# Memory keys by pairs of features, products of zeros at the start, and a fixed TensorE order in the first stage of an encoder kernel

## The chip, the cores and the metric

The kernel runs on one core of a Trainium2 chip. The metric is the device time of one execution in microseconds (us). A core has five engines that run side by side, each through its own list of instructions in order: PE (TensorE, matrix products; PEld is its weight load), DVE (VectorE), ACT (ScalarE), POOL (GpSimd) and SP (SyncE, which here only issues transfers). Transfers run on 16 DMA engines that all queues share. Data lives in SBUF, products accumulate in eight PSUM banks of 128 x 512 numbers.

## The reference, cut to what matters

One layer of an encoder on two sequences of 512 tokens (`x_prompt`, `x_sample`, 1024 features), each with its own memory of 256 tokens.

```
xn = rmsnorm(x, norm_mix);  mn = rmsnorm(mem, norm_mem)
u, q, k, v, xq, g = split(xn @ w_in)
y_s5   = s5_branch(u, lambda, log_step, b, c, ...)      # state-space scan in both directions
y_diff = diff_attention(rope(q), rope(k), v)
mk, mv = split(mn @ w_mem_kv)                           # keys and values of the memory
y_x    = cross_attention(xq, mk, mv)
merged = sum_n sigmoid(g_n) * (branch_n @ w_up[n])
x = x + merged @ w_out
x = x + ffn(rmsnorm(x));  out = rmsnorm(x)
```

All of it is float32. The change touches only what comes first: `mk`, `mv`, the norm of `x`, the product that gives `u`, and the small coefficients of the S5 branch (powers of exp(lambda * step) and the scaled `b`).

## The kernel before, in words

**Number format.** Every large product is done in three: an operand is split into a high part (a cast, ACT, line 122 or 125) and a low part (what is left, DVE, line 123 or 126), and `hi*hi + hi*lo + lo*hi` is accumulated. `weight` (131-137) loads 512 KB of weights into `wf` (two buffers), and `split` makes `wh` and `wl` (two buffers each). `mm3` (141-149) issues the three products of one 128-row slice. All PE instructions of the main program have line 55 (products) or 58 (transposes), since they pass through the class `InOrder`; while its flag `on` is set, each instruction it issues is held to the order of the program.

**Who sets the order.** The Tile framework plans at compile time the order of each engine's list with a simulated clock: an instruction that is ready goes, and among ready ones the earlier in the program. `tc.issue_after(ins)` puts what its block issues behind `ins` on `ins`'s engine. `queued()` (270) does so behind the last weight transfer on SP, `yielding(sp)` (275) behind a split's cast on ACT and its subtraction on DVE.

**First stage, lines 204-335.** The memory arrives transposed in four tiles `mt` of two feature slices each (`mem_part`, 210), is scaled and split into `mh`, `ml`. The keys come head by head: `mem_k(h, w)` (245) needs all eight feature slices and one weight tile, adds 24 products in one PSUM bank of the tag "tr", and ACT copies the bank out (line 252). The weights `w_mk` are laid out for that by `_mtiles` (1413). The values come by pairs of features: `mem_v(c, w)` (257) needs one `mh`/`ml` tile and one weight tile for 24 products into four banks of the tag "mm", kept open over four calls.

Beside them the norm of `x` is prepared. `sums` (216) loads tokens (`tk`) and lets ACT square and add them (line 223). `factor` (183) takes the root on ACT (186) and the reciprocal on DVE (187), and spreads it with four PE transposes (190, shown with line 58) over a "tr" bank. `x_norm` (233) makes `xh` and `xl` from it, with three instructions for each of 16 slices (lines 237-239).

**S5.** `s5_gen` is a generator; each `next(s5)` issues a part of it. Its second part loads `lr`, `li`, `ls` (1110-1112). Its third, issued at line 336 behind `uw`, loads `br`, `bi`, `cr`, `cn` (1116-1119), computes the small coefficients in some 90 DVE instructions on 128 x 32 numbers (1080-1199), and then the input weights (`cprod` on DVE 1237-1239, transposes on PE 1251). After the products of `u` (line 350, banks "mm") come the output weights (PE 1283), the state inputs (PE 1312), the scan of 62 steps on DVE (1327-1330) and the outputs (PE 1355-1357), which line 376 puts behind the twelfth gate product on PE. Gate products (`gates`, 361) fill PE meanwhile.

The first lines of the stage's order:

```python
mem_part(0)
mw = [weight(a["w_mk"][0])]
for i in range(1, 4):
    mem_part(i)
mw.append(weight(a["w_mk"][1]))
with queued():
    next(s5)
    ss0 = sums(a["xN"][0], ts=range(3))
mem_k(0, mw[0])
```

Of the kernel before, what the change touches and what calls it, by code (L numbers as in the profile page):

```python
# [19 lines left out]
P = 128  # L20
L = 512
# [40 lines left out]
def encoder(ctx: ExitStack, tc: tile.TileContext, a, out):  # L62
# [4 lines left out]

    cst = ctx.enter_context(tc.tile_pool(name="cst", bufs=1))
    edge = ctx.enter_context(tc.tile_pool(name="edge", bufs=1, side="right"))
    V.memset(edge.tile([P, 248], F32, name="pad_r"), 0.0)  # L70
# [23 lines left out]
    def slot(tag, shape=(P, NT), dt=F32, name="sl"):  # L94
        return pools[tag].tile(list(shape), dt, tag=tag, name=name)
# [4 lines left out]
    def aux():  # L100
        return bank("tr")


    ident = cst.tile([P, P], F32, name="ident")
    nc.sync.dma_start(ident, a["ident"])
    vec = cst.tile([P, N_VEC], F32, name="vec")
    nc.sync.dma_start(vec, a["vecs"])
    onec = cst.tile([P, 2], F32, name="onec")
# [5 lines left out]
    def vcol(name, i=0):  # L114
        o = VEC[name][0] + i
        return vec[:, o : o + 1]


    def split(hi, lo, src, scale=None):

        if scale is None:
            h = S.copy(hi, src)  # L122
            l_ = V.tensor_tensor(out=lo, in0=src, in1=hi.bitcast(F32), op=ALU.subtract)  # L123
        else:
            h = S.activation(out=hi, in_=src, func=AF.Copy, scale=scale)
            l_ = V.scalar_tensor_tensor(out=lo, in0=src, scalar=scale, in1=hi.bitcast(F32), op0=ALU.mult, op1=ALU.subtract)
        return h, l_
# [54 lines left out]

    def factor(ss, n, nt=4, bias=epsc):

        rs = rp.tile([P, 4], F32, tag="rs", name="rs", bufs=4)
        S.activation(out=rs[:, :nt], in_=ss[:, :nt], func=AF.Sqrt, scale=1.0 / n, bias=bias)
        V.reciprocal(rs[:, :nt], rs[:, :nt])
        bc = aux()
        for t in range(nt):
            PE.transpose(bc[:, t * P : (t + 1) * P], rs[:, t : t + 1].broadcast_to([P, P]), ident)  # L190
        return rs, bc

# [17 lines left out]
    def mem_part(i):  # L210
        mt_ = slot("ld", [P, 2, L], name="mt")
        nc.sync.dma_start(mt_, a["memT"][:, 2 * i : 2 * i + 2, :])
        for j in range(2):
            split(mh[i][:, j, :], ml[i][:, j, :], mt_[:, j, :], scale=vcol("norm_mem", 2 * i + j))

    def sums(src, tag="wb", ss=None, ts=range(4)):

# [22 lines left out]

    mhk = [mh[i // 2][:, i % 2, :] for i in range(KD)]
    mlk = [ml[i // 2][:, i % 2, :] for i in range(KD)]
    mf = None

    def mem_k(h, w):
        nonlocal mf
        o = aux()
        for i in range(KD):
            mm3([o], *w, [(mhk[i], mlk[i])], i, KD)
        if h % 2 == 0:  # L250
            mf = slot("ld", [P, 2, L], name="mf")
        S.copy(mf[:, h % 2], o)
        return mf

    ob = []
# [24 lines left out]
    mem_part(0)  # L280
    mw = [weight(a["w_mk"][0])]
    for i in range(1, 4):
        mem_part(i)
    mw.append(weight(a["w_mk"][1]))
    with queued():
        next(s5)
        ss0 = sums(a["xN"][0], ts=range(3))
    mem_k(0, mw[0])
    mw.append(weight(a["w_mk"][2]))
    with queued():  # L290
        sums(a["xN"][0], ss=ss0, ts=(3,))
        x_load(0, range(2))
    mf0 = mem_k(1, mw[1])
    mw.append(weight(a["w_mk"][3]))
    with queued():
        x_load(0, range(2, 4))
        ss1 = sums(a["xN"][1], ts=range(1))
    _, bc = factor(ss0, DM)
    with yielding(last_s):
        x_norm(0, bc, range(2))  # L300
    mem_k(2, mw[2])
    mw.append(weight(a["w_mv"][0]))
    with queued():
        sums(a["xN"][1], ss=ss1, ts=range(1, 4))
    with yielding(last_s):
        x_norm(0, bc, range(2, 6))
    mf1 = mem_k(3, mw[3])
    mw.append(weight(a["w_mv"][1]))
    with queued():
        x_load(1)  # L310
    with yielding(last_s):
        x_norm(0, bc, range(6, 8))
        _, bc = factor(ss1, DM)
        x_norm(1, bc, range(2))
    mem_v(0, mw[4])
    mw.append(weight(a["w_mv"][2]))
    with yielding(last_s):
        x_norm(1, bc, range(2, 6))
    s5_from = last_s
    mem_v(1, mw[5])  # L320
    mw.append(weight(a["w_mv"][3]))
    with queued():
        nc.sync.dma_start(mD[0], mf0)
        nc.sync.dma_start(mD[1], mf1)
    with yielding(last_s):
        x_norm(1, bc, range(6, 8))
    mem_v(2, mw[6])
    mem_v(3, mw[7])
    for s in range(NS):
        mf = slot("ld", [P, 2, L], name="mf")  # L330
        for j in range(2):
            S.copy(mf[:, j], ob[2 * s + j])
        nc.sync.dma_start(mD[2 + s], mf)
    uw = [weight(a["w_in"][t]) for t in range(2)]
    with tc.issue_after(s5_from[0].ins):
        next(s5)

# [4 lines left out]
    for t2 in range(2):  # L342
        if t2:
            uw = [weight(a["w_in"][2 + t]) for t in range(2)]
        us = [slot("ld", [P, T, NS, NC], name="ut") for _ in range(2)]
        for s in range(NS):
            for t in range(2):
                o = bank()
                for k in range(KD):
                    mm3([o], *uw[t], [x_of(k, s)], k, KD)  # L350
                S.copy(us[t][:, :, s, :], o.rearrange("p (j c) -> p j c", c=NC))
        for t in range(2):
            nc.sync.dma_start(uD[(2 * t2 + t) * P : (2 * t2 + t + 1) * P], us[t])
# [742 lines left out]
def s5_gen(k):  # L1096
# [14 lines left out]
    nc.sync.dma_start(li, a["lam_im"])  # L1111
    nc.sync.dma_start(ls, a["log_step"])
    yield
    br, bi = pp.tile([P, G, 16], F32, name="br"), pp.tile([P, G, 16], F32, name="bi")
    cr, cn = cp.tile([P, G, 16], F32, name="cr"), cp.tile([P, G, 16], F32, name="cn")
    nc.sync.dma_start(br, a["b_re"])
    nc.sync.dma_start(bi, a["b_im"])
    nc.sync.dma_start(cr, a["c_re"])
    nc.sync.dma_start(cn, a["c_im"])

    def sm(nm, n=G):
        return pp.tile([P, n], F32, tag="m_" + nm, name=nm)
# [75 lines left out]
    V.tensor_tensor(out=gr, in0=gr, in1=dn, op=ALU.mult)  # L1198
    V.tensor_tensor(out=gi, in0=gi, in1=dn, op=ALU.mult)


    V.tensor_scalar_mul(cn, cn, -1.0)
    b_r, b_i = cp.tile([P, G, 16], F32, name="b_r"), cp.tile([P, G, 16], F32, name="b_i")
# [196 lines left out]
def layout(i):  # L1400
    i = {k_: np.asarray(v_) for k_, v_ in i.items()}
    a = {}
    x = np.stack([_tok(i["x_prompt"][0]), _tok(i["x_sample"][0])])
    a["xT"] = x.reshape(NS, L, KD, P).transpose(0, 3, 2, 1)
    mem = np.concatenate([i["mem_prompt"][0], i["mem_sample"][0]])
    a["xN"] = x.reshape(NS, 4, P, DM)
    a["memN"] = mem.reshape(4, P, DM)
    a["memT"] = mem.reshape(2 * NMEM, KD, P).transpose(2, 1, 0)
    w = i["w_in"][0]
    a["w_in"] = _mtiles(w)  # L1410
    a["w_v"] = np.stack([_moving(w[:, 1536 + 256 * h : 1792 + 256 * h], 4) for h in range(2)])
    wk = i["w_mem_kv"][0]
    a["w_mk"] = _mtiles(wk[:, :512])
    a["w_mv"] = _moving(wk[:, 512:], 2)
    a["w_glu"] = _mtiles(i["s5_w_glu"][0])
    a["w_up"] = np.stack([_mtiles(i["w_up"][0, n]) for n in range(3)])
    a["w_out"] = _mtiles(i["w_out"][0])
    a["w_fg"] = _mtiles(i["w_ffn_in"][0][:, :FF])
    a["w_fu"] = _mtiles(i["w_ffn_in"][0][:, FF:])
    a["w_fo"] = _mtiles(i["w_ffn_out"][0])  # L1420
    vecs = {"norm_mix": i["norm_mix"][0], "norm_mem": i["norm_mem"][0], "norm_ffn": i["norm_ffn"][0],
            "norm_final": i["norm_final"], "s5_d": i["s5_d"][0], "s5_b_glu": i["s5_b_glu"][0],
            "diff_subln": i["diff_subln"][0]}
# [35 lines left out]
```

## Time and profile before

| what | value |
|---|---|
| three runs | 1651.36, 1651.90, 1654.61 us; median 1651.9 us |
| the profiled execution | 1650.99 us, of which the span from first to last instruction is 1649.3 us |
| busy in the span | PE 98%, PEld 82%, DVE 65%, ACT 38%, POOL 24% |
| granted TensorE clock | 0.993 on the mean |
| moved by DMA | 197.68 MB |

The span differs from the profiled execution by 1.7 us around it, and that execution lies 0.9 us under the median. PE is the engine to watch: a stretch in which it has nothing to do, or runs its products more slowly, is lost, unless a later wait gives it back. A row of the timeline gives start, duration, engine, line, operation, output<-inputs and, in brackets, the idle time before it and what ended that. A row with "xN" merges N instructions. Products on PE overlap, so their rate is read from starts, not from durations.

### The profile page before, as it was taken

Reading aid. Unit: us, or ns where it says so; the run is one execution under the profiler, and the core shown is the slowest. Engines: PE = TensorE matmul, PEld = TensorE weight load, DVE = VectorE, ACT = ScalarE, POOL = GpSimd, SP = SyncE. Lnnn points to the kernel's source line nnn. Section 1 sums busy time; section 2 is a strip of 40 time slices with the busy share of each in tenths; the row PEclk is TensorE's granted clock in tenths of the full one; section 3 lists DMA queues with packets and bytes.
Section 4 is the critical chain, followed back from the end, with each engine's and each line's share of the span. In section 5 each row is a group of like instructions: output and inputs, shape, how many; then the busy total and the mean of one; then the engine's idle time right before and its main releaser. Section 6 shows DMA issues by size and latency. Waiting matters only on the chain.

```text
span 1649.3 us, 20987 instructions
## 1 busy us (share of the span) xinstructions
PE 1608.7 (98%) x7916; PEld 1348.2 (82%) x7916; DVE 1071.1 (65%) x1732; ACT 619.0 (38%) x1082; POOL 397.9 (24%) x253
## 2 busy tenths in 40 slices
PE   7999999999999999999999989999999999999997
PEld 5788788788898889888878868888888888788887
DVE  7957897245555776876465568777777777742324
ACT  6534323235443456564123342232323233521121
POOL 0001100000001221300443345555545552400021
PEclk9999999999999999999999999999999999999999
DMA  9354343736111321155453522322222223731202
GB/s 366 122 166 151 109 156 116 229 125 230 64 45 59 89 72 52 58 182 172 145 186 120 153 77 103 115 77 81 86 89 77 89 78 125 267 114 54 82 11 103
DMA packets 79653, 197.68 MB, mean 120 GB/s; under 512 B 11457, under 2 KB 27073, under 8 KB 79553
## 3 DMA queue, kind: packets, MB, share of 16 engines
q1 hardware_dynamic: 79552, 196.36, 35.3%
q8 instruction: 62, 1.02, 0.3%
q14 instruction: 39, 0.31, 0.1%
HBM read 141.82 MB, written 50.30 MB: 116 GB/s over the span
## 4 chain that ended last, share of the span: by engine, by line
PE 83%; DVE 7%; issue 3%; ACT 3%; DMA 2%; POOL 2%; SPq 1%; DVEq 0%; POOLq 0%; ACTq 0%
PE bkmm L55 74%; PE bksc L55 2%; PE bkoo L55 2%; PE bktr L55 2%; PE bktr L58 1%; DVE wl L123 1%; PE bktr L1312 1%; POOL mg L679 1%; DVE st L1330 1%; ACT e L427 1%; PE bktr L1283 1%; DMA c_n<-cD 1%; DMA yt<-bD 0%; DVE xt L237 0%; ACT wh L122 0%
## 5 line engine op out<-in xcount | busy, mean ns | idle before, releaser
L122 ACT CAST wh<-wf 128x1024 fp32r<-128x1024 f32 (+4 forms) x164 | 142.1, 867 | 391.7 <-PE bkmm L55 360.5
L55 PE MATMUL bkmm<-xh,wh 128*128 128x512 f32 x640 | 253.6, 396 | 1.9 <-ACT wh L122 1.2
L55 PE MATMUL bkmm<-xh,wl 128*128 128x512 f32 x640 | 251.4, 393 | 2.3 <-DVE wl L123 2.3
L55 PE MATMUL bkmm<-xl,wh 128*128 128x512 f32 x640 | 251.1, 392 | 0.0
L55 PE MATMUL bkmm<-tl,wh 128*128 128x512 f32 x612 | 239.8, 392 | 3.9 <-DVE tl L123 3.9
L55 PE MATMUL bkmm<-th,wh 128*128 128x512 f32 x612 | 239.5, 392 | 0.0
L55 PE MATMUL bkmm<-th,wl 128*128 128x512 f32 x612 | 237.9, 390 | 0.0
L123 DVE TENSOR_TENSOR wl<-wf,wh 128x1024 fp32r<-128x1024 f32 (+4 forms) x164 | 174.3, 1063 | 81.3 <-ACT wh L122 76.7
L55 PE MATMUL bkmm<-ah,wh 128*128 128x512 f32 (+1 forms) x408 | 147.2, 361 | 0.0
L55 PE MATMUL bkmm<-al,wh 128*128 128x512 f32 (+1 forms) x408 | 147.2, 361 | 0.0
L55 PEld LDWEIGHTS bkmm<-xh,wl 128*128 128x128 f32 x640 | 120.6, 188 | 29.5 <-DVE wl L123 3.1
L55 PEld LDWEIGHTS bkmm<-xh,wh 128*128 128x128 f32 x640 | 120.7, 189 | 25.8 <-ACT wh L122 1.8
L55 PEld LDWEIGHTS bkmm<-xl,wh 128*128 128x128 f32 x640 | 120.7, 189 | 23.3 <-issue 0.4
L55 PEld LDWEIGHTS bkmm<-tl,wh 128*128 128x128 f32 x612 | 115.4, 189 | 29.1 <-DVE tl L123 5.4
L55 PEld LDWEIGHTS bkmm<-th,wh 128*128 128x128 f32 x612 | 115.5, 189 | 23.9
L55 PEld LDWEIGHTS bkmm<-th,wl 128*128 128x128 f32 x612 | 115.2, 188 | 23.9
L632 POOL TENSOR_TENSOR t<-t,rs 128x512 f32<-128x512 f32 x16 | 24.2, 1511 | 456.6 <-DVE t L631 415.7
L55 PE MATMUL bkmm<-ah,wl 128*128 128x512 f32 (+1 forms) x408 | 127.5, 361 | 1.0 <-DVE wl L123 1.0
L991 POOL TENSOR_TENSOR up<-up,acc 128x512 f32<-128x512 f32 x44 | 85.0, 1954 | 148.1 <-DVE up L967 148.1
L1051 DVE TENSOR_TENSOR y<-y,bkmm 128x512 f32<-128x512 f32 (+1 forms) x56 | 32.6, 608 | 111.8 <-PE bkmm L55 111.8
L170 POOL TENSOR_TENSOR acc<-acc,nsq 128x512 f32<-128x512 f32 (+1 forms) x32 | 37.9, 1186 | 243.8 <-ACT nsq L169 243.6
L55 PEld LDWEIGHTS bkmm<-ah,wl 128*128 128x128 f32 x408 | 76.9, 189 | 13.2 <-DVE wl L123 1.8
(587 smaller groups left out, 3244.5 us busy)
## 6 DMA issues: line engine op xcount, KB each, us to landing
wf<-in_w_in SPq DMA_DIRECT2D x40, 512.0 KB, 3.8
gD<-gt SPq DMA_DIRECT2D x24, 512.0 KB, 2.8
gl<-gD SPq DMA_DIRECT2D x24, 512.0 KB, 3.7
wf<-in_w_fg SPq DMA_DIRECT2D x22, 512.0 KB, 3.6
wf<-in_w_fu SPq DMA_DIRECT2D x22, 512.0 KB, 3.6
aD<-ac SPq DMA_DIRECT2D x22, 512.0 KB, 2.6
fl<-aD SPq DMA_DIRECT2D x22, 512.0 KB, 4.5
wf<-in_w_fo SPq DMA_DIRECT2D x16, 448.0 KB, 3.2
```

The source lines that it names most:

```text
L55: return self.put(self.eng.matmul(*args, **kw))
L58: return self.put(self.eng.transpose(*args, **kw))
L122: h = S.copy(hi, src)
L123: l_ = V.tensor_tensor(out=lo, in0=src, in1=hi.bitcast(F32), op=ALU.subtract)
L170: eng.tensor_tensor(out=acc[:, :n], in0=acc[:, :n], in1=sq[:, :n], op=ALU.add)
L427: S.activation(out=e, in_=sc, func=AF.Exp, bias=nb, scale=scale, accum_out=sm)
L632: PO.tensor_tensor(out=t2, in0=t2, in1=rope[1], op=ALU.mult)
L679: PO.tensor_tensor(out=mg[m], in0=mg[m], in1=gt, op=ALU.add)
L991: PO.tensor_tensor(out=up, in0=up, in1=accs[s], op=ALU.mult)
L1051: V.tensor_tensor(out=y[m][:, c : c + n], in0=y[m][:, c : c + n], in1=o_, op=ALU.add)
L1283: PE.matmul(kp[64 * hf : 64 * hf + 48, g * 144 : (g + 1) * 144], l_[:, 2 * hf + g, :], o_[:, 4 * g4 + 2 * hf + g, :], start=(l_ is lr48), ...
L1312: PE.matmul(ps[:, g * P : (g + 1) * P], w_[:, gg * P : (gg + 1) * P], u_[:, 8 * o + gg, :], start=True, stop=True)
```

## The change

- **Keys by pairs of features.** `mem_k` now works as `mem_v` does: one call needs one `mh`/`ml` tile and one weight tile, and adds 24 products into four "tr" banks that stay open over four calls. `w_mk` is laid out by `_moving`. Within a feature slice the order is: four heads with `wh`, `mh`; four with `wh`, `ml`; four with `wl`, `mh`. The number of products is the same, 96. The four banks are copied out by `mem_out` behind the last call.
- **First loads.** The first `mt` tile and the first weight tile are loaded and split in halves, alternately. `ident` is no longer the first transfer; it goes behind the second weight tile. The memory's third and fourth tiles are loaded later, behind two token tiles.
- **Products of zeros.** Six products of the zero tile `pad_r` (128 x 248, float32) go into a "tr" bank ahead of the first real product. Nothing reads them.
- **Fixed order.** `PE.on` is set over the whole stage, up to the weights of `u`.
- **Norm.** `factor` is divided in `root` and `spread`. The first spread stands behind `mem_k(3)`, the second behind `mem_v(1)`.
- **S5.** The small coefficients are issued behind `mem_k(3)`, the loads of `br`, `bi`, `cr`, `cn` behind the seventh weight tile (`w_mv[2]`), and the rest where it was.
- **Banks of `u`.** The first two products of `u` use "tr" banks.

```diff
-    nc.sync.dma_start(ident, a["ident"])
...
+    def mem_k(c, w):
+        wh, wl = w
+        if c == 0:
+            kb.extend(aux() for _ in range(4))
+        for kk in range(2):
+            kt = 2 * c + kk
+            for w_, x_ in ((wh, mhk), (wh, mlk), (wl, mhk)):
+                for h, o in enumerate(kb):
+                    PE.matmul(o, w_[:, kk * L + h * P : kk * L + (h + 1) * P], x_[kt], start=(kt == 0 and x_ is mhk and w_ is wh),
+                              stop=(kt == KD - 1 and w_ is wl))
+    def mem_out(i, banks):
+        mf = slot("ld", [P, 2, L], name="mf")
+        for j in range(2):
+            S.copy(mf[:, j], banks[j])
+        return mf
...
+    PE.on = True
+    idle = aux()
+    for _ in range(6):
+        PE.matmul(idle[:, :248], pad_r[:, :P], pad_r, start=True, stop=True)
...
+    mem_load(0, (slice(0, 1), slice(1, 2)))
+    mem_load(1)
+    mem_weight(a["w_mk"][1])
     with queued():
+        nc.sync.dma_start(ident, a["ident"])
         next(s5)
-        ss0 = sums(a["xN"][0], ts=range(3))
+        ss0 = sums(a["xN"][0], ts=range(2))
+    mem_load(2)
     mem_k(0, mw[0])
-    mw.append(weight(a["w_mk"][2]))
+    mem_weight(a["w_mk"][2])
+    mem_load(3)
+    mem_k(1, mw[1])
+    mem_weight(a["w_mk"][3])
     with queued():
-        sums(a["xN"][0], ss=ss0, ts=(3,))
-        x_load(0, range(2))
-    mf0 = mem_k(1, mw[1])
+        sums(a["xN"][0], ss=ss0, ts=range(2, 4))
+    mem_k(2, mw[2])
+    mem_weight(a["w_mv"][0])
     with queued():
+        x_load(0)
+    rs0 = root(ss0, DM)
+    mem_k(3, mw[3])
+    next(s5)
     with yielding(last_s):
-        x_norm(0, bc, range(2))
+        mfs = [mem_out(i, kb[2 * i : 2 * i + 2]) for i in range(2)]
+        bc = spread(rs0)
+        x_norm(0, bc, range(4))
+    mem_weight(a["w_mv"][1])
     with queued():
+        ss1 = sums(a["xN"][1])
+    mem_v(0, mw[4])
     with yielding(last_s):
+        x_norm(0, bc, range(4, 8))
+    mem_weight(a["w_mv"][2])
+    s5_from = last_s
     with queued():
+        x_load(1, range(2))
+        next(s5)
+    mem_v(1, mw[5])
+    bc = spread(root(ss1, DM))
     with yielding(last_s):
+        x_norm(1, bc, range(4))
+    mem_weight(a["w_mv"][3])
...
+    mem_v(2, mw[6])
     with yielding(last_s):
+        x_norm(1, bc, range(4, 8))
     mem_v(3, mw[7])
...
     uw = [weight(a["w_in"][t]) for t in range(2)]
+    PE.on = False
...
-                o = bank()
+                o = bank() if t2 or s else aux()
...
-    a["w_mk"] = _mtiles(wk[:, :512])
+    a["w_mk"] = _moving(wk[:, :512], 2)
```

More of the change, by code (lines that the diff above doesn't have):

```diff
@@ L69, in encoder @@
     edge = ctx.enter_context(tc.tile_pool(name="edge", bufs=1, side="right"))
-    V.memset(edge.tile([P, 248], F32, name="pad_r"), 0.0)
+    pad_r = edge.tile([P, 248], F32, name="pad_r")
+    V.memset(pad_r, 0.0)
     wp = ctx.enter_context(tc.tile_pool(name="wp", bufs=2))
@@ L183, in factor, with root @@
     def factor(ss, n, nt=4, bias=epsc):
+        rs = root(ss, n, nt, bias)
+        return rs, spread(rs, nt)
+    def root(ss, n, nt=4, bias=epsc):
         rs = rp.tile([P, 4], F32, tag="rs", name="rs", bufs=4)
@@ L187, in factor, with spread @@
         V.reciprocal(rs[:, :nt], rs[:, :nt])
+        return rs
+    def spread(rs, nt=4):
         bc = aux()
@@ L190, in factor @@
             PE.transpose(bc[:, t * P : (t + 1) * P], rs[:, t : t + 1].broadcast_to([P, P]), ident)
-        return rs, bc
+        return bc
     open_banks(mm=4, tr=4)
@@ L208, in encoder @@
     ml = [slot("it" if i else "mem", [P, 2, L], F32R, f"ml{i}") for i in range(4)]
[L210 to L214, printed above, removed]
     def sums(src, tag="wb", ss=None, ts=range(4)):
@@ L242, in encoder @@
     mlk = [ml[i // 2][:, i % 2, :] for i in range(KD)]
[L243 to L252, printed above, removed]
+    kb = []
+    def mem_k(c, w):
[12 more added lines that the diff above has]
+            S.copy(mf[:, j], banks[j])
         return mf
@@ L278, in yielding, with mem_load @@
             yield
[L280 to L284, printed above, removed]
+    PE.on = True
+    idle = aux()
+    for _ in range(6):
+        PE.matmul(idle[:, :248], pad_r[:, :P], pad_r, start=True, stop=True)
+    wf = wp.tile([P, DM], F32, tag="wf", name="wf")
+    mw = [tuple(wp.tile([P, DM], F32R, tag=n_, name=n_) for n_ in ("wh", "wl"))]
+    def mem_load(i, parts=(slice(0, 2),)):
+        mt_ = slot("ld", [P, 2, L], name="mt")
+        for js in parts:
+            nc.sync.dma_start(mt_[:, js], a["memT"][:, 2 * i + js.start : 2 * i + js.stop, :])
+            if i == 0:
+                ws_ = slice(js.start * L, js.stop * L)
+                nc.sync.dma_start(wf[:, ws_], a["w_mk"][0, :, ws_])
+            for j in range(js.start, js.stop):
+                split(mh[i][:, j, :], ml[i][:, j, :], mt_[:, j, :], scale=vcol("norm_mem", 2 * i + j))
+            if i == 0:
+                split(*(w_[:, ws_] for w_ in mw[0]), wf[:, ws_])
@@ L285, in encoder, with mem_weight @@
+    def mem_weight(src):
+        mw.append(weight(src))
+    mem_load(0, (slice(0, 1), slice(1, 2)))
+    mem_load(1)
+    mem_weight(a["w_mk"][1])
     with queued():
+        nc.sync.dma_start(ident, a["ident"])
         next(s5)
-        ss0 = sums(a["xN"][0], ts=range(3))
+        ss0 = sums(a["xN"][0], ts=range(2))
+    mem_load(2)
     mem_k(0, mw[0])
-    mw.append(weight(a["w_mk"][2]))
+    mem_weight(a["w_mk"][2])
+    mem_load(3)
+    mem_k(1, mw[1])
+    mem_weight(a["w_mk"][3])
     with queued():
-        sums(a["xN"][0], ss=ss0, ts=(3,))
-        x_load(0, range(2))
@@ L293, in encoder @@
-    mf0 = mem_k(1, mw[1])
-    mw.append(weight(a["w_mk"][3]))
+        sums(a["xN"][0], ss=ss0, ts=range(2, 4))
+    mem_k(2, mw[2])
+    mem_weight(a["w_mv"][0])
     with queued():
-        x_load(0, range(2, 4))
-        ss1 = sums(a["xN"][1], ts=range(1))
-    _, bc = factor(ss0, DM)
+        x_load(0)
+    rs0 = root(ss0, DM)
+    mem_k(3, mw[3])
+    next(s5)
     with yielding(last_s):
-        x_norm(0, bc, range(2))
-    mem_k(2, mw[2])
-    mw.append(weight(a["w_mv"][0]))
+        mfs = [mem_out(i, kb[2 * i : 2 * i + 2]) for i in range(2)]
+        bc = spread(rs0)
+        x_norm(0, bc, range(4))
@@ L303, in encoder @@
+    mem_weight(a["w_mv"][1])
     with queued():
-        sums(a["xN"][1], ss=ss1, ts=range(1, 4))
+        ss1 = sums(a["xN"][1])
+    mem_v(0, mw[4])
     with yielding(last_s):
-        x_norm(0, bc, range(2, 6))
-    mf1 = mem_k(3, mw[3])
-    mw.append(weight(a["w_mv"][1]))
+        x_norm(0, bc, range(4, 8))
+    mem_weight(a["w_mv"][2])
+    s5_from = last_s
     with queued():
-        x_load(1)
+        x_load(1, range(2))
+        next(s5)
+    mem_v(1, mw[5])
+    bc = spread(root(ss1, DM))
@@ L311, in encoder @@
     with yielding(last_s):
[L312 to L316, printed above, removed]
-    with yielding(last_s):
[L318 to L327, printed above, removed]
+        x_norm(1, bc, range(4))
@@ L328, in encoder @@
+    mem_weight(a["w_mv"][3])
+    with queued():
+        x_load(1, range(2, 4))
+        for i in range(2):
+            nc.sync.dma_start(mD[i], mfs[i])
+    mem_v(2, mw[6])
+    with yielding(last_s):
+        x_norm(1, bc, range(4, 8))
     mem_v(3, mw[7])
     for s in range(NS):
[L330 to L333, printed above, removed]
+        nc.sync.dma_start(mD[2 + s], mem_out(2 + s, ob[2 * s : 2 * s + 2]))
@@ L1113, in s5_gen @@
     yield
[L1114 to L1119, printed above, removed]
     def sm(nm, n=G):
@@ L1199, in s5_gen @@
     V.tensor_tensor(out=gi, in0=gi, in1=dn, op=ALU.mult)
+    yield
+    br, bi = pp.tile([P, G, 16], F32, name="br"), pp.tile([P, G, 16], F32, name="bi")
+    cr, cn = cp.tile([P, G, 16], F32, name="cr"), cp.tile([P, G, 16], F32, name="cn")
+    nc.sync.dma_start(br, a["b_re"])
+    nc.sync.dma_start(bi, a["b_im"])
+    nc.sync.dma_start(cr, a["c_re"])
+    nc.sync.dma_start(cn, a["c_im"])
+    yield
     V.tensor_scalar_mul(cn, cn, -1.0)
```

## The prediction

> **What bounds the kernel now.** I read the page first for the shares of the engines, then PE's list of waits in the first 70 us, then the timelines of PE, ACT, DVE and SP there, and last the stretch around 272 to 301 us, where S5 ends.
>
> ```profile
> PE 1608.7 (98%) x7916; PEld 1348.2 (82%) x7916; DVE 1071.1 (65%) x1732; ACT 619.0 (38%) x1082; POOL 397.9 (24%) x253
> ...
> PE bktr L55 <- ACT wh L122: 8.0, 1, 8.0
> PE bktr L58 <- DVE rs L187: 3.5, 1, 3.5
> PE bkmm L55 <- DVE wl L123: 1.3, 3, 0.5
> PE bkmm L55 <- ACT wh L122: 1.2, 1, 1.2
> ```
>
> PE is busy 98% of the span, so only a stretch in which it stands still or runs slowly can be won. 1649.3 - 1608.7 = 40.6 us are idle in all; the four rows of waits (total, times, longest) put 14.0 us of that before 70 us. The timeline adds what the list can't show, a slow pace:
>
> ```profile
> 7.97 0.80 PE L55 MATMUL bktr<-mh,wh 128*128 128x512 f32 x1 [7.97 <-ACT wh L122]
> ...
> 12.26 0.40 PE L55 MATMUL bktr<-mh,wh 128*128 128x512 f32 x1
> ...
> 21.04 0.39 PE L55 MATMUL bktr<-mh,wl 128*128 128x512 f32 x1
> 24.97 0.65 PE L58 MATMUL bktr<-ident,rs 128*128 128x128 f32 x4 [3.54 <-DVE rs L187]
> 25.37 0.48 PE L55 MATMUL bktr<-mh,wh 128*128 128x512 f32 x1
> ...
> 29.33 0.40 PE L55 MATMUL bktr<-ml,wh 128*128 128x512 f32 x1
> ...
> 62.65 0.39 PE L55 MATMUL bkmm<-xh,wh 128*128 128x512 f32 x1
> ...
> 64.44 0.50 PE L55 MATMUL bkmm<-xh,wh 128*128 128x512 f32 x1 [1.17 <-ACT wh L122]
> ```
>
> From 12.26 to 21.04 there are 38 steps, 0.231 us each: the full pace. From 7.97 to 12.26 there are nine steps in 4.29 us, where 2.08 would do: 2.2 us lost. From 25.37 to 29.33, behind a pause, ten steps take 3.96 us where 2.31 would do: 1.65 us lost. The pause itself, from the end of the pace at 21.27 to 24.97, is 3.7 us: the planner had put the spread of the first norm ahead of the third head's products. So before the products of `u` run freely at 64.44 the losses are 7.97 + 2.2 + 3.7 + 1.65 + 1.3 + 1.2 = **18.0 us**. The other part, 192 products of 0.23 us (44.2 us) and two spreads of 0.4 us (24.97 to 25.37), is work that stays.
>
> **The change part by part.** *Start.* What comes first on each engine:
>
> ```profile
> 0.74 0.39 SPq L105 DMA_DIRECT2D ident<-in_ident  x1
> 1.18 0.42 SPq L107 DMA_DIRECT2D vec<-in_vecs  x1
> 1.65 0.42 SPq L212 DMA_DIRECT2D mt<-in_memT  x1
> 2.12 0.43 SPq L134 DMA_DIRECT2D wf<-in_w_mk  x1
> ...
> 5.12 1.33 ACT L125 ACTIVATE mh<-mt,vec 128x512 fp32r<-128x512 f32 x2 [2.89 <-DMA mt<-in_memT]
> 6.88 1.04 ACT L122 CAST wh<-wf 128x1024 fp32r<-128x1024 f32 x1 [0.43 <-DMA wf<-in_w_mk]
> ...
> 0.85 0.27 DVE L70 MEMSET pad_r<- 128x248 f32 x1 [0.85 <-PEq L1452]
> ...
> 5.00:10.00 5.00, 3.91 (x6) 1.00 1.00 372
> ...
> 302.44 0.64 PE L1356 MATMUL bktr<-x,c_r 128*128 128x128 f32 x2
> 302.87 0.64 PE L1357 MATMUL bktr<-x,c_n 128*128 128x128 f32 x2
> ```
>
> The first `mt`, 512 KB, is issued at 1.65 and there at 5.12: 3.47 us. At the 372 GB/s of 5 to 10 us (last column), 512 KB take 1.41 us, so 2.06 us are latency. Now `ident`'s place falls away (0.44 us) and the halves are 256 KB, 0.70 us each: issued at 1.18, the half of `mt` is there at 3.94, that of `wf` at 4.64. Half a cast, about 0.6 us of the 1.04, lets the first real product go at 5.3. The zeros begin when `pad_r` is set, at 1.12. A float32 product of 128 columns steps 0.43 us at the slow pace (302.44 to 302.87), one of 248 columns then 0.83, and six 5.0, to 6.1; if the pace doubles after 4.29 us as it did from 7.97 on, they end at 5.8. I take **6.0** for the first real product, and full pace from it. Bounds: 5.4, if the zeros never hold it up, and 7.1, if a half takes as long as the whole (3.47 us to land, then 6.88 - 5.12 = 1.76 for the weights' half, a cast of 0.6). If zeros don't lift the pace, 2.2 us more.
>
> The Trainium skill, "TensorE: Matmul & The Clock Gate", section "What's actually happening", says that PE runs at half rate until a free-running window of about 3.4 us was busy. The two slow stretches above (4.29 and 3.96 us) agree; as the window is free-running, the zeros might end before it does, which by that rule would cost about 1 us at most.
>
> The page "DMA: Bandwidth & Descriptors" of the Trainium skill, section "Measured (HBM→SBUF, 128 partitions, SWDGE, issued from GpSimd)", speaks against halves: 64 KB in 0.95 us, 1 MB in 6.15. Between these an estimate for 256 KB is 2.0 us, and the first real product would come at about 7.9, a sum 1.9 us worse; the trace's 372 GB/s were moved in transfers of 512 KB, and no row here shows a half.
>
> *Supply of the keys.* By pairs, PE needs one tile and one weight tile per 24 products (5.5 us):
>
> ```profile
> L122 ACT CAST wh<-wf x10: 1043/1048/1054, 6.9 to 63.3; 128x1024 fp32r<-128x1024 f32 x10
> L123 DVE TENSOR_TENSOR wl<-wf,wh x10: 1217/1224/1229, 8.0 to 68.4; 128x1024 fp32r<-128x1024 f32 x10
> ...
> L125 ACT ACTIVATE mh<-mt,vec x8: 706/714/727, 5.1 to 11.8; 128x512 fp32r<-128x512 f32 x8
> L126 DVE SCALAR_TENSOR_TENSOR ml<-mt,vec,mh x8: 744/746/752, 5.9 to 12.6; 128x512 fp32r<-128x512 f32 x8
> ...
> L252 ACT COPY mf<-bktr 128x512 f32<-128x512 f32 x4 | 2.3, 587 | 8.6 <-PE bktr L55 8.6
> ```
>
> A pair costs ACT 1.05 + 2 x 0.71 = 2.5 us and DVE 1.22 + 2 x 0.75 = 2.7 us, under 5.5. Its 1 MB takes 2.8 us at 372 GB/s. The third pair waits on SP behind the S5 loads and two token tiles: 4.3 MB lie up to the end of its weights (1.05 in halves, 1.05 second pair, 0.14 `vec`, `ident` and S5, 1.05 tokens, 1.05 third pair), 11.6 us from 3.2, so 14.8. The cast is done at 15.9 and the subtraction at 17.1; PE wants the one at 6.0 + 11.0 = 17.0 and the other eight products later, 18.8. Cover 1.1 us, nothing lost; if transfers run slower, it costs the difference. I keep 0.6 us (0 to 1.3) for waits on splits, as now. The four key banks' copies lie beside `mem_v(0)`; the first spread needs one bank free, and in fixed order all of PE waits behind it. The first bank's last product is the fourth from the end (0.69 us before it), a copy takes 0.59: **0.4 us** (0 to 1.0).
>
> *The pause.* The spread stands behind 96 products, at about 28 us. Its four token tiles are issued ahead of `w_mv[0]`, which PE wants only then, so 3.7 and 1.65 us go. What is late next is DVE:
>
> ```profile
> 0.00:21.40 21.40, 13.39 (x48) 10.04 (x48) 15.31 (x64) 13.71 (x20) 0.66 (x6) 1.00 0.90 340
> 21.40:38.00 16.60, 13.06 (x53) 10.66 (x53) 12.43 (x60) 8.92 (x14) 0.00 (x0) 0.90 1.03 414
> 38.00:62.65 24.65, 23.35 (x101) 18.22 (x100) 24.65 (x39) 21.82 (x49) 0.00 (x0) 1.00 0.45 156
> ```
>
> The columns behind PE and PEld are DVE and ACT. DVE works 52.4 us up to 62.65 and is full in the last stretch; that is why weight splits come late there. The change adds nothing to it and moves the small coefficients ahead of `x_norm` and the loads of `br` to `cn` behind them. From its first subtraction at about 4.7 DVE can't be through all of that before 57.1. PE reaches `u` at 6.0 + 44.2 + 0.8 + 1.0 = 52.0. What is left then is not all due (the second sequence is wanted 11 us later), but its `x_norm` stands ahead of `u`'s first split. So of the 1.2 us wait ahead of `u` I keep **1.5** (0 to 3.0).
>
> *Sum.* Losses after: 6.0 + 0 + 0.4 + 0.6 + 1.5 = 8.5 us, against 18.0: **9.5 us won**. Bounds: 5.4 gives 12.6 won; 7.1 + 2.2 + 1.0 + 1.3 + 3.0 = 14.6 gives 3.4. The profiled execution, 1650.99, would become 1641.5; the median of the runs lies 0.9 above it, so **1642.4 us** from 1651.9.
>
> *Given back later?* S5:
>
> ```profile
> 98.10 1.23 DVE L1237 TENSOR_TENSOR ct<-cr,xr__696 128x1024 f32<-128x1024 f32 x1
> 108.66 1.23 DVE L123 TENSOR_TENSOR wl<-wf,wh 128x1024 fp32r<-128x1024 f32 x1 [9.33 <-ACT wh L122]
> ...
> 113.13 0.45 PE L1283 MATMUL bktr<-cxr,lr 128*48 128x144 f32 x4
> ...
> 272.56 0.39 DVE L1330 TENSOR_TENSOR st<-p__2308,q__2309 128x128 f32<-128x128 f32 x1
> ...
> 274.39 0.39 PE L55 MATMUL bkmm<-xh,wl 128*128 128x512 f32 x1
> ...
> 301.38 0.46 PE L1355 MATMUL bktr<-u__1194,w__2734 128*128 128x128 f32 x2 [3.40 <-DMA w__2734<-gD]
> ```
>
> The scan's last step (272.56) and the twelfth gate's last product (274.39) end together, and the outputs need both. The scan must thus move forward with PE. Its chain starts with PE's line 1283 at 113.13, behind `u`; DVE had its part ready at 99.33 and then stood 9.33 us. With PE there at 103.6, DVE is still in time by 4.3 us without getting any faster. So the gain should last.
>
> **The rivals.**
>
> 1. *The fixed order stops PE at the second spread.* It needs the second norm:
>
> ```profile
> 46.14 0.17 DVE L187 RECIPROCAL rs<-rs 128x4 f32<-128x4 f32 x1
> ```
>
> PE arrives behind 144 products, at about 40.0. For it: nothing may pass the spread. Against: the token tiles are issued in one go behind `w_mv[1]`. If the norm came no earlier than now (46.3), PE would stand 6.3 us and run slowly for 1.65; DVE would use that, so the 1.5 goes: 15.0 lost, 3.0 won, 1648.9. It decides from a reciprocal later than 40.
>
> 2. *The start does not do what it says:* the zeros don't lift the pace (2.2) and a half takes as long as a whole (7.1). Then 11.8 are lost, 6.2 won: 1645.7. For it: no row shows zeros or a half. Against: nothing in the rows ties the pace to values.
>
> 3. *The stall at 301.38 goes too,* because everything is planned anew: 3.4 and a slow stretch like the 1.65 above, 5.0 more: 1637.4. Against: it is a transfer, which nothing here touches.
>
> 4. *Slower: the scan does not follow.* If DVE's cross products for S5 end later, behind `x_norm` and the late `br` to `cn`, line 1283 and the scan slip, and PE runs out of gates ahead of the outputs. Each microsecond past 103.6 costs one; from 9.5 of slip on nothing is won, from 13 on the kernel is slower by more than can be confused; a slip of 15 gives 1657.4. For it: scan and gates end within 2 us of each other. Against: the idle 9.33, and gates that PE could draw forward.
>
> **How the numbers follow.** Forecast 0.60; rival 1 0.12; rival 2 0.12; rival 3 0.06; rival 4 0.10, of which 0.07 past the point of slower. A measurement tells 0.2% (3.3 us) from no change. Faster: 0.60 + 0.12 + 0.06 + half of rival 1 = 0.84; same 0.06 + 0.03 = 0.09; slower 0.07. The range from 1637.0 to 1649.5 takes in the bounds of the sum, rival 2, nearly all of rival 1 and about half of rival 3: 0.85.
>
> **What would show it.** The first product with `mh` near 6.0 at a step of 0.23 from the start; no wait on `rs` over 1 us; the first product of `u` near 52; line 1283 near 104; the scan's last step near 263. Wrong: steps of 0.43 behind the zeros (rival 2), a wait of several us at line 58 (rival 1), a long wait at line 1355 or gates exhausted ahead of it (rival 4).

## The result, and the profile after it

| | before | after |
|---|---|---|
| median of ten runs each | 1653.45 us | 1657.22 us |
| lowest to highest | 1651.36 to 1654.79 | 1654.03 to 1660.17 |
| profiled span | 1649.3 us | 1654.4 us |

The changed kernel is slower: ratio 1.0022, with a 95% interval from 1.0013 to 1.003, which is at the edge of the 0.2% that can be told from no change. The 9.5 us that were to be won are gone, and 3.8 us more (1657.22 - 1653.45). The first question is whether the stage itself went as forecast. PE's waits in the first 110 us (total, times, longest):

```profile
PE bktr L1285 <- DVE cxr L1273: 6.1, 2, 3.5
PE bktr L1285 <- DVE cxi L1273: 2.5, 3, 1.5
PE bkmm L55 <- DVE wl L123: 2.2, 2, 1.2
PE bktr L58 <- DVE rs L191: 1.9, 1, 1.9
```

The 8.0 us for the first weights and the 3.5 us ahead of the first spread, both in the list of before, are gone. In their place stand two rows that the list of before does not have: line 1285, the S5 transposes, waits for DVE's cross products. Two windows of 50 us separate the two halves of the story. The columns are busy time of PE, PEld, DVE, ACT and POOL with instructions, then granted clock, DMA share and GB/s. First the kernel before:

```profile
0.00:50.00 50.00, 38.01 (x151) 29.89 (x152) 39.74 (x143) 33.45 (x57) 0.66 (x6) 0.97 0.88 333
50.00:100.00 50.00, 47.97 (x234) 39.19 (x233) 47.24 (x48) 23.72 (x48) 1.55 (x3) 1.00 0.40 139
```

and the same windows of the changed kernel:

```profile
0.00:50.00 50.00, 45.66 (x189) 35.30 (x189) 41.34 (x144) 38.28 (x70) 0.66 (x6) 1.00 0.93 349
50.00:100.00 50.00, 39.29 (x183) 31.78 (x183) 44.80 (x49) 18.51 (x35) 2.78 (x3) 0.90 0.30 105
```

Busy time alone misleads before 50 us: PE is busy 7.65 us more there, but 4.29 us of that are the products of zeros. The instructions (the numbers with x) tell more. PE issues 38 more before 50 us; 12 of them are the six products of zeros (the trace shows two rows for each), and the other 26, 6.0 us at the full pace of 0.23 us each, are the gain. Between 50 and 100 us PE is busy 8.68 us less and issues 51 instructions fewer, which is the loss. PE's timeline shows where:

```profile
1.18 4.29 PE L55 MATMUL bktr<-pad_r 128*128 128x248 f32 x12 [1.18 <-DVE pad_r L71]
5.61 1.20 PE L55 MATMUL bktr<-mh,wh 128*128 128x512 f32 x4
...
43.60 0.65 PE L58 MATMUL bktr<-ident,rs 128*128 128x128 f32 x4 [1.88 <-DVE rs L191]
...
56.73 0.39 PE L55 MATMUL bkmm<-xh,wh 128*128 128x512 f32 x1
...
68.85 1.03 PE L1285 MATMUL bktr<-ident,cxr 128*128 128x128 f32 x8
70.31 1.06 PE L1285 MATMUL bktr<-ident,cxi 128*128 128x128 f32 x8 [0.43 <-DVE cxi L1273]
74.85 1.06 PE L1285 MATMUL bktr<-ident,cxr 128*128 128x128 f32 x8 [3.48 <-DVE cxr L1273]
77.37 1.94 PE L1285 MATMUL bktr<-ident,cxi 128*128 128x128 f32 x8 [1.45 <-DVE cxi L1273]
81.91 1.94 PE L1285 MATMUL bktr<-ident,cxr 128*128 128x128 f32 x8 [2.60 <-DVE cxr L1273]
84.43 1.92 PE L1285 MATMUL bktr<-ident,cxi 128*128 128x128 f32 x8 [0.58 <-DVE cxi L1273]
86.02 0.56 PE L55 MATMUL bktr<-xh,wh 128*128 128x512 f32 x1
...
97.65 0.45 PE L1317 MATMUL bktr<-cxr,lr 128*48 128x144 f32 x4
...
119.56 0.45 PE L1317 MATMUL bktr<-cxi,li 128*48 128x144 f32 x4
```

(Line 1285 is the old 1251, line 1317 the old 1283.) The first real product comes at 5.61, the first product of `u` at 56.73, 5.9 us earlier than before. That first product is of the second sequence (banks "mm"). Behind 48 of those stand all six blocks of transposes in a row, with nothing between them, and only then the first product of `u` in a "tr" bank, at 86.02. Waits inside that block are 0.43 + 3.48 + 1.45 + 2.60 + 0.58 = 8.5 us, and the last three groups of eight take 1.9 us where the first three take 1.05, 2.6 us more: 11.1 us. The granted clock says the same of the second half of the block:

```profile
68.85:77.37 8.52, 3.16 (x26) 2.54 (x24) 8.42 (x9) 3.22 (x6) 0.00 (x0) 0.92 0.00 0
77.37:86.02 8.65, 5.47 (x24) 4.73 (x25) 8.58 (x8) 2.76 (x5) 1.15 (x1) 0.50 0.00 0
```

DVE is busy throughout (8.42 of 8.52, 8.58 of 8.65): it makes one pair of cross products per 7.06 us (74.85 to 81.91), and PE has nothing else that it may do. The DMA columns are zero: SP issues no weight transfer from 61.5 to 93.97, and DVE splits no weights between its rows at 59.93 and 92.72, since the next tiles need the buffers that the waiting products of `u` still hold. Weights are late afterwards too: DVE later stands idle for 15.67 us, here in its own timeline of the changed kernel:

```profile
115.09 1.23 DVE L123 TENSOR_TENSOR wl<-wf,wh 128x1024 fp32r<-128x1024 f32 x1 [15.67 <-ACT wh L122]
...
278.56 0.39 DVE L1364 TENSOR_TENSOR st<-p__2319,q__2320 128x128 f32<-128x128 f32 x1
```

The scan ends at 278.56, where it ended at 272.56 before and was forecast for about 263. The 6.0 us by which it is late are those of line 1317: four of its rows come early, at 97.65, but the rest only at 119.56, where they came at 113.41 before.

**Why the transposes stand there.** Each transposed group of the input weights takes a "tr" bank: three `o`, two tiles, two halves, 12 banks. They are issued by `next(s5)` in the lines directly ahead of `u`. With `o = bank() if t2 or s else aux()` the two products of the first sequence ask for the thirteenth and fourteenth bank of the same rotating tag. This is theory A: a bank goes to who asked first in the program, so these 48 products of `u` cannot start until the transposes have, however ready they are. Before the change they had "mm" banks, and the planner could put them between the transposes. The rival, theory B, put the loss on the S5 parts that were moved forward.

### The profile page after: what moved, and what is told of

It reads as the page before. It is cut to its first block, busy times and chain, and to the rows that moved or that the text cites. A ratio compares the mean times of both kernels' runs of the same rounds, so it can differ in the third digit from the quotient of the medians.

```text
span 1654.4 us, 21012 instructions
## 1 busy us (share of the span) xinstructions
PE 1612.4 (97%) x7928; PEld 1349.2 (82%) x7928; DVE 1069.7 (65%) x1733; ACT 619.6 (37%) x1083; POOL 398.8 (24%) x253
## 4 chain that ended last, share of the span: by engine, by line
PE 79%; DVE 11%; issue 3%; DMA 3%; ACT 2%; POOL 2%; SPq 1%; DVEq 0%; POOLq 0%; ACTq 0%
PE bkmm L55 70%; PE bksc L55 2%; PE bktr L55 2%; PE bkoo L55 2%; PE bktr L58 1%; DVE wl L123 1%; DVE st L1364 1%; PE bktr L1346 1%; POOL mg L711 1%; DMA c_n<-cD 1%; DMA yt<-bD 1%; ACT e L459 1%; DVE xt L238 1%; DVE ct L1271 0%; DVE tl L123 0%
## 5 line engine op out<-in xcount | busy, mean ns | idle before, releaser
L55 PE MATMUL bkmm<-xh,wl 128*128 128x512 f32 x624 | 244.0, 392 | 3.5 <-DVE wl L123 3.5
L55 PE MATMUL bkmm<-xh,wh 128*128 128x512 f32 x624 | 246.6, 395 | 0.7 <-ACT gt L556 0.7
L55 PE MATMUL bkmm<-xl,wh 128*128 128x512 f32 x624 | 244.1, 391 | 0.0
L55 PEld LDWEIGHTS bkmm<-xh,wl 128*128 128x128 f32 x624 | 117.2, 188 | 30.0 <-DVE wl L123 4.8
L55 PEld LDWEIGHTS bkmm<-xh,wh 128*128 128x128 f32 x624 | 117.3, 188 | 23.9 <-ACT gt L556 1.1
```

Of the source, the lines that this page charges most:

```text
L55: return self.put(self.eng.matmul(*args, **kw))
```

## The experiments

Each time stands beside that of the kernel before, measured together with it; "won" is the difference of these two medians. Where two changed kernels are compared that were not measured together, their gains over the kernel before are compared.

**1. `u_mm`: the changed kernel with all products of `u` in "mm" banks.**

```diff
-                o = bank() if t2 or s else aux()
+                o = bank()
```

> The changed kernel with one line taken back: the first two products of u use banks of the tag mm again, as before the change. Theory A (the bank line): in the changed kernel these two stand in the order of the tr banks behind S5's twelve, so PE stands at S5's six transposes until DVE has made all of them; without the line PE is not at rest between 69.6 and 86.0 us beyond the 5.2 us of the transposes, which is 11.2 us: 1657.2 - 11 = 1646, at most 1 us more for the copies of the value banks. Theory B (DVE is late for S5, because small work and late loads were moved): the transposes still wait for the same cross products, 1655 to 1658. Theory C (the fixed order of the stage or the starved start costs it): no change, 1657.

Measured: 1643.75 us against 1651.73, ratio 0.9948 (0.9936 to 0.9961): 8.0 us won. That is near the 1646 of theory A, while B and C had 1655 or more. The list of PE's waits up to 130 us has no row for line 1285 any more. PE's timeline:

```profile
5.99 1.19 PE L55 MATMUL bktr<-mh,wh 128*128 128x512 f32 x4
...
8.84 1.07 PE L55 MATMUL bktr<-mh,wh 128*128 128x512 f32 x4
...
27.29 1.09 PE L55 MATMUL bktr<-mh,wl 128*128 128x512 f32 x4
28.36 0.65 PE L58 MATMUL bktr<-ident,rs 128*128 128x128 f32 x4
...
42.05 0.65 PE L58 MATMUL bktr<-ident,rs 128*128 128x128 f32 x4 [1.88 <-DVE rs L191]
...
55.20 0.39 PE L55 MATMUL bkmm<-xh,wh 128*128 128x512 f32 x1
...
56.74 0.50 PE L55 MATMUL bkmm<-xh,wl 128*128 128x512 f32 x1 [0.93 <-DVE wl L123]
...
70.93 1.04 PE L1285 MATMUL bktr<-ident,cxr 128*128 128x128 f32 x8
72.74 1.04 PE L1285 MATMUL bktr<-ident,cxi 128*128 128x128 f32 x8
```

Here the groups of transposes wait for nothing: products of `u` lie between them. The scan ends at 264.81. One line of the change took back the whole gain of the others, and 3.8 us more.

**2. `before_tr`: the kernel before, with that line alone.**

```diff
-                o = bank()
+                o = bank() if t2 or s else aux()
```

> The kernel before with that one line alone added: the first two products of u use tr banks. Theory A: PE has only the second sequence's 48 products of u (to about 74 us) and must then stand until the third pair of cross products (89.6 us), less 5.2 us of transposes, so some 9 us slower: 1662 (1659 to 1666). Theories B and C: the line is harmless, 1653.5 within 2.

Measured: 1662.3 us against 1651.73, ratio 1.0062 (1.0049 to 1.0076): 10.6 us lost. Its waits show the same row:

```profile
PE bktr L1251 <- DVE cxi L1239: 5.6, 2, 3.0
```

So the line costs about the same in both surroundings, 10.6 us here and 3.8 + 8.0 = 11.8 us between the changed kernel and `u_mm`; the 11.1 us read from the block above lie between these. No other part of the change is needed for it.

**3. `s5_old`: the changed kernel with the S5 parts back behind the weights of `u`.** 

```diff
     mem_k(3, mw[3])
-    next(s5)
...
         x_load(1, range(2))
-        next(s5)
...
-        next(s5)
+        for _ in range(3):
+            next(s5)
```

> The changed kernel with S5's small work and its four loads issued where they were before, behind the first weights of u. Theory A: the block of transposes ahead of u's first two products stays, 1655 to 1661. Theory B: DVE makes the norm of x first and S5 as before the change, the wait at the transposes goes: at most 1650.

Measured: 1660.66 us against 1651.73, ratio 1.0049 (1.0034 to 1.0064). Theory B falls: putting S5 back wins nothing.

```profile
PE bktr L1284 <- DVE cxi L1272: 6.1, 2, 3.5
PE bkmm L55 <- DVE wl L123: 5.1, 3, 2.4
```

The block is as it was, and waits for `wl` have grown from 2.2 to 5.1 us.

**4. `u_tr_late`: the "tr" banks are kept, but the S5 part with the transposes is issued behind the first half of `u`.**

```diff
-    with tc.issue_after(s5_from[0].ins):
-        next(s5)
...
+        if t2 == 0:
+            with tc.issue_after(s5_from[0].ins):
+                next(s5)
```

> The changed kernel with the tr banks kept for the first two products of u, but S5's part with the transposes issued behind the first half of u. Theory A: it is only the place in the order of the tr banks, so this wins what taking the line back wins, or a little more, since u need not wait for the copies of the value banks: 1643 to 1647. Theory B: DVE still makes its cross products late, and the transposes wait: 1653 or more.

Measured: 1648.46 us against 1651.73, ratio 0.9976 (0.9967 to 0.9985): 3.3 us won. That is 1.5 us outside what theory A had expected (1643 to 1647), and 4.7 us behind `u_mm`, but far from theory B's 1653. Now the same banks are asked for in the other order, and the 50 us window has PE busy again:

```profile
50.00:100.00 50.00, 48.98 (x237) 40.73 (x238) 39.54 (x43) 19.03 (x35) 1.69 (x2) 1.00 0.35 116
```

So the block is not a cost of "tr" banks as such, but of who stands ahead in them. The place behind `u` has a price of its own: DVE does 4.1 us less in this window than in `u_mm` (43.61), S5 comes later, the scan ends at 271.53 and the outputs pay; PE's waits from 130 to 330 us:

```profile
PE bktr L1391 <- ACT x L1382: 6.5, 1, 6.5
```

**5 to 8. The parts of the change, one undone at a time from `u_mm`.**

*`mm_nozero`*: without the six products of zeros.

```diff
-    idle = aux()
-    for _ in range(6):
-        PE.matmul(idle[:, :248], pad_r[:, :P], pad_r, start=True, stop=True)
```

> The kernel u_mm (changed kernel, first products of u in mm banks; 7.98 us faster than the kernel before in its call) without the six products of zeros. Theory D (the zeros lift the pace in time): the first real product comes at about 5.4 instead of 6.0, but nine or ten products run at 0.43 us, 2.2 us lost, so 1.6 us less is won: 6.4 us faster than before. Theory E (the zeros buy nothing, as the pace would be late data's anyway): the same 8 us within 0.5.

Measured: 1642.75 us against 1650.85, ratio 0.9952 (0.9937 to 0.9966). PE's timeline shows what the zeros do:

```profile
5.64 2.08 PE L55 MATMUL bktr<-mh,wh 128*128 128x512 f32 x4 [5.64 <-ACT wh L122]
7.51 1.91 PE L55 MATMUL bktr<-ml,wh 128*128 128x512 f32 x4
...
10.77 1.08 PE L55 MATMUL bktr<-mh,wh 128*128 128x512 f32 x4
```

Twelve products take 5.13 us where `u_mm` takes 2.85 for the same twelve. Those 2.3 us are seen again at the first output-weight product (107.77, in `u_mm` 105.42) and at the scan's end (267.07, in `u_mm` 264.81), but not in the time.

*`mm_free`*: without the fixed order (`PE.on` never set).

```diff
-    PE.on = True
...
-    PE.on = False
```

> The kernel u_mm without the fixed order of TensorE in the stage: the planner puts the first spread behind 19 products of the first value block, and the second behind 33 more. Theory F (the pause of 3.7 us went because the keys come by pairs and the norm is early, the fixed order is not needed): 8 us faster than before within 1.5; the second spread may wait 1.9 us longer or shorter. Theory G (the fixed order carries the gain): at least 3 us less is won, 5 or under.

Measured: 1644.92 us against 1650.85, ratio 0.9962 (0.9947 to 0.9977): 5.9 us won. That lies between the two theories (8 within 1.5, or 5 and under). The wait at the spread goes, and one for `wl` comes:

```profile
PE bkmm L55 <- DVE wl L123: 3.3, 2, 2.7
```

The interval overlaps that of `u_mm`, so what the fixed order is worth, about 2 us by the medians, is not settled.

*`mm_whole`*: the first memory and weight tiles loaded and split whole.

```diff
-    mem_load(0, (slice(0, 1), slice(1, 2)))
+    mem_load(0, (slice(0, 2),))
```

> The kernel u_mm with the first memory tile and the first weight tile loaded whole instead of in halves. By the rows of before (3.47 us to land for a whole tile, 1.76 more for the weights, 1.05 for the cast) the first real product comes at 7.5 instead of 6.0: 1.5 us less is won, 6.5. If halves land no earlier than wholes, or the zeros cover it, 8.0 as u_mm.

Measured: 1647.23 us against 1650.85, ratio 0.998 (0.997 to 0.9989): 3.6 us won, less than expected.

```profile
1.18 5.33 PE L55 MATMUL bktr<-pad_r 128*128 128x248 f32 x12 [1.18 <-DVE pad_r L71]
8.57 2.07 PE L55 MATMUL bktr<-mh,wh 128*128 128x512 f32 x4 [2.07 <-ACT wh L122]
...
13.86 1.25 PE L55 MATMUL bktr<-mh,wh 128*128 128x512 f32 x4
```

The product comes 2.6 us later, and twelve products take 5.29 us. The zeros did not lift the pace here: they take 5.33 us, where in the changed kernel the same six take 4.29, so they ran slowly to their end, 2.07 us ahead of the first real product. The expectation had only the later start and no slow pace. Whether more zeros would cover the gap was not tried.

*`mm_s5old`*: S5's parts back in their old place, the edit of `s5_old`.

> The kernel u_mm with S5's small work and its loads issued behind the first weights of u, where they were before the change. Theory A without rest: with the mm banks S5's transposes no longer stand ahead of u, so the place of the small work is worth little: 8 us faster than before within 1.5. Theory H (DVE must have the small work early, or the scan starts later): 3 us or more is lost of it, 5 or under.

Measured: 1647.92 us against 1650.85, ratio 0.9982 (0.9973 to 0.9992): 2.9 us won. Up to 130 us, and from 130 to 330 us:

```profile
PE bkmm L55 <- DVE wl L123: 4.2, 3, 1.7
```

```profile
PE bktr L1388 <- DMA w__2745<-gD: 5.2, 1, 5.2
```

That is theory H. The early place of S5's parts is thus worth about 5 us: with it, PE waits less for `wl` ahead of and in `u`, and the scan ends earlier (at 264.81 in `u_mm`, at 268.43 here). With "tr" banks it is as much (3.8 us lost by the changed kernel, 8.9 by `s5_old`). The prediction had no term for it: it took the order of the small coefficients for neutral, since DVE's whole work stays the same.

Against the 8.0 us of `u_mm`, undoing the four parts costs -0.1, 2.1, 4.4 and 5.1 us. That is over 11 us together, so the parts lean on each other and their prices cannot be added. Two parts were not undone alone: the keys by pairs of features and the place of the first spread.

**9 to 11. Once more the base, a later second spread, and the zeros again,** measured together.

*`u_mm_again`* is `u_mm`.

> The changed kernel with all products of u in banks of the tag mm, once more, as the base for the two others of this call. It was 8.0 us faster than the kernel before (ratio 0.9948, from 0.9936 to 0.9961), so 1643 to 1645 us where the kernel before takes 1652.

Measured: 1643.68 us against 1651.37, ratio 0.9957 (0.9944 to 0.9971).

*`mm_late`*: the second spread and `x_norm` behind `mem_v(2)`.

```diff
-    bc = spread(root(ss1, DM))
-    with yielding(last_s):
-        x_norm(1, bc, range(4))
+    rs1 = root(ss1, DM)
...
+    bc = spread(rs1)
     with yielding(last_s):
-        x_norm(1, bc, range(4, 8))
+        x_norm(1, bc, range(8))
```

> As u_mm_again, but the second spread and the second sequence's x_norm stand behind mem_v(2), 24 products (5.5 us) later. In u_mm PE waited 1.88 us there for the reciprocal (line 191), and then 0.93 us for wl ahead of the second product of u. DVE was busy for all of 38 to 55 us (17.00 of 17.00). Theory F: the wait is a matter of the order on PE alone; it goes, u is reached 1.9 us earlier, and the kernel is 1.5 to 2.5 us faster than u_mm_again. Theory G: DVE limits the stage from 38 us on; the wait goes at the spread and comes back ahead of u at wl or xl (line 123 or 240), 1.5 to 2.5 us longer than the 0.93, and the time stays within 0.7 us of u_mm_again.

Measured: 1646.62 us against 1651.37, ratio 0.9972 (0.9961 to 0.9984): 4.7 us won, 2.9 us less than the base.

```profile
PE bkmm L55 <- ACT wh L122: 3.3, 2, 1.7
PE bkmm L55 <- DVE wl L123: 1.5, 1, 1.5
```

The wait at the spread is gone, and 3.3 us for `wh` ahead of `u` have come. Theory F falls: the order on PE is not what limits here. Theory G comes nearer, since the wait comes back ahead of `u`, but it named DVE's split and the late one is ACT's, and the kernel is 2.9 us behind the base where G said 0.7 at the most (the intervals overlap). ACT's timeline in this kernel leads back to DVE all the same: ACT stands 3.32 us, up to 52.22, for DVE's scaled `x` (line 238). Casts of `x` and copies of the value banks then stand ahead of its casts of `u`'s weights, which start at 55.27 and 57.73; in `u_mm` they start at 52.94 and 56.31.

*`mm_nozero_again`*:

> As u_mm_again, but without the six products of zeros, a second time. The first time PE's first output-weight product came 2.35 us later than in u_mm and the span was 1.2 us longer, but the time did not differ. Theory D: the zeros are worth the slow pace of the first products, 1.6 to 2.4 us slower than u_mm_again. Theory E: their gain is given back behind the S5 stage; within 0.7 us of u_mm_again.

Measured: 1645.34 us against 1651.37, ratio 0.9963 (0.995 to 0.9975): 1.7 us slower than the base beside it, where the first pair had it 0.1 us the other way (8.1 won against 8.0). The intervals overlap both times, so between D and E nothing is decided. What is shown is the slow pace of the first products without zeros: twelve take 5.20 us here (from 5.96 to 11.16).

## Why the prediction was wrong, point by point

**The failed step is the line "Banks of `u`",** which the section on the change lists and the prediction never costed. Its section "Given back later?" asked only whether line 1283 and the scan follow PE, and concluded "So the gain should last" from DVE being in time. It did not ask what stands between the last product of `mem_v` and line 1283 on PE, and in which order. The runs put 10.6 us (`before_tr`) to 11.8 us (against `u_mm`) on that line alone. A look at who else takes "tr" banks between there would have shown the twelve of line 1251. Line 1283 was also too weak a sign: its first row came at 97.65, ahead of the 104 that was to show the gain, and the scan was late even so.

**Rival 4 had the slip, not its cause.** It priced a slip of 15 us at 1657.4; the scan ended 15.6 us past the forecast 263, and the time was 1657.22. The fit of the time is partly luck: the price was 5.5 us above the 1651.9 of the three runs, and the measured loss is 3.8 us above 1653.45. And it expected DVE's cross products to end later. They ended earlier; the last of the six, in the kernel before and in the changed one:

```profile
88.33 1.22 DVE L1239 TENSOR_TENSOR cxi<-ct,cxi 128x1024 f32<-128x1024 f32 x1
```

```profile
83.06 1.23 DVE L1273 TENSOR_TENSOR cxi<-ct,cxi 128x1024 f32<-128x1024 f32 x1
```

DVE was 5.3 us ahead of its old time, and PE still lost, because the bank order made PE stand at five of the six transposes (waits of 0.43 to 3.48 us).

**The rest of the sum held within 2 us.** `u_mm` is the change without the failed step, and can be laid beside the terms:

| term | forecast | `u_mm` |
|---|---|---|
| first real product | 6.0 (5.4 to 7.1) | 5.99 |
| slow pace behind it | 0 | 0 (12 products from 5.99 to 8.84) |
| bank copy ahead of the first spread | 0.4 | 0.15 (28.36 - 27.29, less 0.92 for four) |
| second spread | 0 (rival 1: 6.3 + 1.65) | 1.88 + 1.56 |
| split waits of the keys | 0.6 | 0 |
| wait ahead of `u` | 1.5 | 0.93 |
| sum | 8.5 | 10.5 |

18.0 - 10.5 = 7.5 us won by the terms; 8.0 and 7.7 were measured, and 9.5 were forecast. So "the gain should last" is true of the rest of the change: the scan's last step moved forward by 7.75 us and the outputs followed. That the first term fits to 0.01 us is luck, since the single terms vary between executions: in the second profile of the same kernel (`u_mm_again`) the first real product comes at 6.74, no slow stretch follows the second spread, and a split wait of 1.22 us stands in its place.

Two slips of the working change nothing: the terms of the late bound for the start add up to 7.0, not 7.1, and the row of DVE at 98.10 already belongs to the next block of output weights, so that its part was ready at 98.1, not 99.33.

**Rival 1 came true in small.** The second norm's reciprocal ended at 42 in `u_mm`, past the 40 from which that rival was to decide, and PE stood 1.88 us. The 1.56 us beside it in the table are a slow stretch behind the pause. A window of `u_mm`, with the granted clock third from the end:

```profile
43.43:46.55 3.12, 3.12 (x8) 2.36 (x8) 3.12 (x8) 3.07 (x11) 0.00 (x0) 0.50 1.02 418
```

3.12 us at half the clock are 1.56 us of PE's time. In the same kernel's second profile the same pause of 1.88 us is followed by the full clock:

```profile
42.67:46.00 3.33, 3.33 (x17) 2.82 (x18) 3.33 (x8) 2.83 (x14) 0.00 (x0) 1.00 1.03 417
```

The Trainium skill, "TensorE: Matmul & The Clock Gate", section "What's actually happening", says that the clock follows PE's activity over a window of about 3.4 us that runs freely and does not start anew with the kernel. The 3.12 us are near its length, and that the same pause is followed by half the clock once and by the full clock once agrees with its running freely. The same section has the clock fall after at least one idle window; here a pause of 1.88 us, about half of one, was enough once, and the measurement decides.

The slow stretch did not delay `u`, though. From the second spread to the first product of `u` PE took 13.15 us with it (42.05 to 55.20) and 13.13 without (42.67 to 55.80), since in the second profile PE waited for DVE's split instead:

```profile
50.38 0.50 PE L55 MATMUL bkmm<-wl,mh 128*128 128x512 f32 x1 [1.22 <-DVE wl L123]
...
55.80 0.39 PE L55 MATMUL bkmm<-xh,wh 128*128 128x512 f32 x1
```

**Rival 2 did not come.** In the eight profiles with halves and zeros the first real product came between 5.61 and 6.74, under the bound of 7.1, and behind it at most about 0.6 us of the 2.2 us of slow pace was lost (1.61 us for four products in `s5_old`, 1.04 in the changed kernel). The Trainium skill, "DMA: Bandwidth & Descriptors", section "Measured (HBM→SBUF, 128 partitions, SWDGE, issued from GpSimd)", had led to an estimate of 2.0 us per half and 7.9 for that product; none of the eight profiles agrees with it.

**Rival 3 is not shown.** In `u_mm` PE waits 2.1 us for the transfer behind the scan, where it waited 3.40 before, but in the second profile of the same kernel it waits 3.5:

```profile
PE bktr L1389 <- DMA w__2745<-gD: 2.1, 1, 2.1
```

```profile
PE bktr L1389 <- DMA w__2745<-gD: 3.5, 1, 3.5
```

## What to carry to other kernels

When a product changes the tag of its buffer, list what else takes buffers of that tag between there and its old neighbours, in the order of the program: a rotating pool is a queue, and whoever asks behind a slow user waits behind it, however ready it is. Moving work forward on an engine is only worth what the next fixed order on it lets through, so after the stage that is changed follow that engine to the next point where it waits for another. A diff is costed line by line; the one that looks like bookkeeping is a line too.

## What the runs showed of the hardware that was not expected

- The slow pace can come back after a short pause: 1.88 us without a product were followed by it once out of two profiles of `u_mm`, and not in the changed kernel, whose pause was as long (43.60).
- The time after which the same products lift the pace varies: the six of zeros, from 1.18 us on, take 4.29 us in the changed kernel and 5.33 us in `mm_whole`.
- The granted clock does not tell of every slow pace. In `mm_nozero` the first twelve products take 5.13 us, and the window over them still shows 1.00:

```profile
5.64:10.77 5.13, 5.13 (x13) 4.02 (x14) 2.90 (x6) 2.94 (x5) 0.00 (x0) 1.00 1.00 351
```

- The start varies between executions of one kernel by about as much as a part of this change is worth: the first real product of `u_mm` came at 5.99 in one profile and at 6.74 in the other, because ACT began on the first half of the memory at 4.71 and at 5.46.
